# Four mixers in a row: the next mixer's norm is spread over the partitions behind the third part of its values, and the output projection's evictions stand behind all weight splits

## The chip, the cores and the metric

The kernel runs on one core of one Trainium2 chip. The metric is the device time of one execution in microseconds (us). TensorE (PE) multiplies, VectorE (DVE) and ScalarE (ACT) do the elementwise work and empty PSUM, GpSimd (POOL) helps, and SyncE (SP) issues nearly all transfers.

## The reference, cut to what matters

A first model of two blocks (mixers and a mixture of experts) is followed by a second one of four mixers in a row. Only the second one is touched by the change:

```python
def second_block(x, norm_pre, norm_post, ...):
    h = x
    for i in range(4):
        u = rms_norm_2(h, norm_pre[i])                     # over the 1024 channels of each of 256 tokens
        y = (nsa_mixer, diff_mixer, dilated_mixer, stick_mixer)[i](u, ...)
        h = h + rms_norm_2(y, norm_post[i])
    return h

def diff_mixer(u, w_in, w_out, ...):                       # the other mixers have the same frame
    q, k, v, z = split_cols(u @ w_in, (1024,) * 4)
    ...                                                    # attention gives o, 256 x 1024
    return (o * jax.nn.silu(z)) @ w_out
```

## The kernel before

All matrices are float32. A product of two float32 matrices is made of three matmuls: each operand is split into a rounded high part and the low rest (`wh` and `wl` for weights, `oh` and `ol`, `rawh` and `rawl` for activations), and high by low, low by high and high by high are added up in PSUM. A weight of 1024 x 256 comes by one transfer of 1 MB (`wload`, L220, a pool of five buffers), and `split` makes its halves: for each half, ACT rounds (L248, the cast `wh<-w`), then DVE subtracts (L249, `wl<-w,wh`). There are four buffers each of `wh` and `wl`, of half a weight each, so that two weights are split at any time, and a cast waits until TensorE has done with the weight that held its buffer.

The 256 tokens lie as two tiles of 128 rows in `h` (`hrow` in the trace). A mixer ends in `out_proj`: four column blocks of 256 of the product with `w_out`, for two row tiles t. Each piece is evicted by ACT (L354, squares summed into `ssq`) and by DVE (L355, times the gain, into `y`); both read the same PSUM bank and so take turns. `norm` makes the scale of a row tile of `ssq` (`rout`: a reduction on DVE, then Ln and Exp on ACT), and `add` puts y times the scale on `h` (L360). The next mixer does not wait for its own norm: `rows_turned` turns the rows into columns on TensorE (L404) and splits the result, times the gain of the next norm, into `rawh` and `rawl` without the row's scale (L409 on ACT, L410 on DVE), first row tile 0. Row tile 1 and the scale itself are made by `next_norm` (kept in `self.rest`), which `values` calls after the first eight of its products.

`values` is the next mixer's first product, v = u @ w (L608), in four column blocks, called the four parts here. The first two parts have their weights ready (`self.ahead`); row tile 0 is done for both before row tile 1. The scale `rc` is put on at the eviction of v (L632, L633). The q, k and z products, which have tokens along the free dimension, need the scale along the free dimension as well, as `rr` and `rq`: `rb` is `rc` spread to 128 columns (L428), two transposes turn it (L431), and two copies take it out of PSUM (L432, L433).

The order of the instructions on each engine is not written out. A scheduler sorts them by a simulated timeline; the code's order and `issue_after(ins)`, which keeps what is traced inside it behind `ins` on the engine of `ins`, constrain it. Within an engine the order is then fixed.

The places where one mixer ends and the next begins are called the three transitions: into `diff` (from about 1107 us), into `dilated` (from about 1261 us) and into `stick` (from about 1396 us). `stick` ends the program with an `out_proj` that writes the output.

Of the kernel before, what the change touches and what calls it, by code (L numbers as in the profile page):

```python
# [11 lines left out]
F32R = mybir.dt.float32r  # L12
BF16 = mybir.dt.bfloat16
I32 = mybir.dt.int32
AF = mybir.ActivationFunctionType
# [4 lines left out]
S = 256  # L20
D = 1024
KT = 8
# [85 lines left out]
class K:  # L108
# [227 lines left out]
    def out_proj(self, pool, oh, ol, w_out, gain, ahead=None, out=None):  # L336

        nc, h = self.nc, self.h  # L340
        y = pool.tile([128, 2, D], F32, name="y", tag="v")
        junk = pool.tile([128, 512], F32, name="ysq", tag="ysq")
        ssq = pool.tile([128, 2, 4], F32, name="ssq")
        r = pool.tile([128, 2], F32, name="rout")

        def product(v, t, w, ks, first=True, last=True):
            for k in ks:
                for j, (o, b) in enumerate(((oh, 1), (ol, 0), (oh, 0))):
                    nc.tensor.matmul(v, o[:, k, 128 * t:128 * t + 128], w[b][k], start=first and k == 0 and j == 0,  # L349
                                     stop=last and k == KT - 1 and j == 2)  # L350

        def evict(v, t, c):
            cs = slice(256 * c, 256 * c + 256)
            nc.scalar.activation(junk[:, :256], v, AF.Square, accum_out=ssq[:, t, c:c + 1])  # L354
            nc.vector.tensor_mul(y[:, t, cs], v, gain[:, cs])  # L355

        def add(t, b):
            cs = slice(512 * b, 512 * b + 512)
            dst = h if out is None else y
            nc.vector.scalar_tensor_tensor(dst[:, t, cs], y[:, t, cs], r[:, t:t + 1], h[:, t, cs], op0=ALU.mult, op1=ALU.add)  # L360
            if out is not None:
                nc.sync.dma_start(out[128 * t:128 * t + 128, cs], y[:, t, cs])

        weights = lambda c: self.wsplit(w_out[:, 256 * c:256 * c + 256], after=self.oh_last if c == 2 else (), pool_too=c == 1)

        half = slice(0, 256), slice(256, 512)
        ws, p = [weights(0), weights(1)], [self.mm(), self.mm()]
        for ks in ((0, 1, 2, 3), (4, 5), (6, 7)):
            for c in range(2):
                for t in range(2):  # L370
                    product(p[t][:, half[c]], t, ws[c], ks, c == 0, c == 1)
        w, q = weights(2), self.pss()
        for ks in ((0, 1, 2, 3), (4, 5, 6, 7)):
            for t in range(2):
                product(q[:, half[t]], t, w, ks, t == 0, t == 1)
        w = weights(3)
        for t in range(2):
            for c in range(2):
                evict(p[t][:, half[c]], t, c)
        for t in range(2):  # L380
            evict(q[:, half[t]], t, 2)
        if ahead is not None:
            self.ahead = [self.wsplit(ahead[0][0])]
            self.raw = [x.tile([128, KT, S], F32R, name=n, tag=n) for x, n in ((self.rawh, "rawh"), (self.ub, "rawl"))]
        p = [self.pss()[:, :256] for _ in range(2)]
        for t in range(2):
            product(p[t], t, w, range(KT))
        for t in range(2):
            evict(p[t], t, 3)
            self.norm(r[:, t:t + 1], ssq[:, t])  # L390
            for b in range(2):
                add(t, b)
                if ahead is not None and t == 0:
                    self.rows_turned(ahead[1], t, b)
        if ahead is not None:
            self.ahead += [self.wsplit(a) for a in ahead[0][1:]]
            self.rest = lambda: self.next_norm(ahead[1])

    def rows_turned(self, gain, t, b):
# [13 lines left out]
    def next_norm(self, gain):  # L413

        nc, h = self.nc, self.h
        for b in range(2):
            self.rows_turned(gain, 1, b)

        self.rc, self.rr, self.rq = (self.hp.tile([128, n], F32, name=t, tag=t) for t, n in (("rc", 2), ("rr", S), ("rq", S)))
        hsq = self.hp.tile([128, 2, 2], F32, name="hsq", tag="hsq")  # L420
        with self.tc.issue_after(self.raw_last[0]):
            for t in range(2):
                for b in range(2):
                    junk = self.ub.tile([128, 2, S], F32, name="rawsq", tag="rawsq", bufs=2)
                    nc.scalar.activation(junk.rearrange("p a b -> p (a b)"), h[:, t, 512 * b:512 * b + 512], AF.Square, accum_out=hsq[:, t, b:b + 1])
                self.norm(self.rc[:, t:t + 1], hsq[:, t])
        rb = self.ub.tile([128, 2, S], F32, name="rb", tag="rawsq", bufs=2)[:, :, :128]
        nc.vector.tensor_copy(rb, self.rc.unsqueeze(2).to_broadcast([128, 2, 128]))  # L428
        p = self.pst()
        for t in range(2):  # L430
            nc.tensor.transpose(p[:, 128 * t:128 * t + 128], rb[:, t], self.ident)  # L431
        nc.scalar.copy(self.rr, p[:, :S])  # L432
        nc.scalar.mul(self.rq, p[:, :S], 0.125)  # L433

    def norm(self, out, parts):

        nc = self.nc
        nc.vector.tensor_reduce(out, parts, axis=mybir.AxisListType.X, op=ALU.add)
        nc.scalar.activation(out, out, AF.Ln, bias=self.eps, scale=1.0 / D)
        nc.scalar.activation(out, out, AF.Exp, scale=-0.5)  # L440

    def normed(self, wk, p, r, n=2):

# [155 lines left out]
    def values(self, parts):  # L599

        nc = self.nc
        x = self.raw
        ps = [self.mm(), self.mm()] + (self.pair() if len(parts) > 2 else [])

        def product(i, w, t, k):
            ts = slice(128 * t, 128 * t + 128)
            for j, (a, b) in enumerate(((0, 1), (1, 0), (0, 0))):
                last = nc.tensor.matmul(ps[i][:, 256 * t:256 * t + 256], x[a][:, k, ts], w[b][k], start=k == 0 and t == 0 and j == 0,  # L608
                                        stop=k == KT - 1 and t == 1 and j == 2).ins
            return last  # L610

        ws = self.ahead
        self.ahead = None

        tiles = range(2)
        order = ([(i, t, k) for t in tiles for i in range(2) for k in range(KT)] if self.by_tile else
                 [(i, t, k) for k in range(KT) for i in range(2) for t in tiles])
        for n, (i, t, k) in enumerate(order):
            if n == KT and self.rest is not None:
                with self.tc.issue_after(last):  # L620
                    self.rest()
                self.rest = None
            last = product(i, ws[i], t, k)
        (last_a, last_b), rc = self.raw_last, self.rc
        for i, (src, v) in enumerate(parts):
            if i > 1:
                with self.tc.issue_after(last_a), self.tc.issue_after(last_b):
                    w = self.wsplit(src)
                for t in tiles:
                    for k in range(KT):  # L630
                        product(i, w, t, k)
            nc.scalar.mul(v[:, 0], ps[i][:, :256], rc[:, 0:1])  # L632
            nc.vector.tensor_scalar(v[:, 1], ps[i][:, 256:], rc[:, 1:2], None, op0=ALU.mult)  # L633

# [600 lines left out]
    def even(self, gs, shift, gate):  # L1235
# [3 lines left out]
        with ExitStack() as ctx:  # L1239
# [71 lines left out]
            with self.pool("eo", 1) as op:  # L1311
                add, norm = self.norms(self.blk, op, 2)
                for c in range(4):
                    w = self.wload(w_out[:, 256 * c:256 * c + 256])
                    with self.tc.issue_after(self.last):
                        w = self.split(w)
                    for m in range(2):
                        k = 2 * c + m
                        p = self.mm()
                        sl = slice(128 * m, 128 * m + 128)  # L1320
                        self.gemm(p, lambda k: w[0][k][:, sl], lambda k: w[1][k][:, sl], lambda k: xs[k // 2][0][:, k % 2], lambda k: xs[k // 2][1][:, k % 2],
                                  (4, 5, 6, 7, 0, 1, 2, 3))
                        for i, dst in ((0, self.x), (1, self.cx)):
                            nc.vector.scalar_tensor_tensor(dst[:, k], p[:, 256 * i:256 * i + 256], gate[:, k, i:i + 1],
                                                           dst[:, k], op0=ALU.mult, op1=ALU.add)
                        add(k, [self.x[:, k], self.cx[:, k]])
                self.r = norm()
# [963 lines left out]
```

## Time and profile before

| what | value |
|---|---|
| median of 3 runs | 1564.4 us (1552.34 to 1564.49) |
| the profiled execution: time, span of its trace | 1566.07 us, 1564.4 us |
| mean granted clock of TensorE over the span | 0.955 |
| PE busy | 1417.6 us (91%) |
| DVE, ACT, POOL busy | 967.4, 807.1, 253.8 us (62%, 52%, 16%) |
| mean transfer rate | 183 GB/s |

Busy time is an average over stages with different limits. What a change in one place is worth is read from the stretch around it: which engine waits there, and for what.

### The profile page before, as it was taken

The numbers are of one execution on the slowest core, as the hardware profiler recorded it, in microseconds if no ns is written. First come the engines' busy times: TensorE is split into PE (matmuls) and PEld (weight loads), VectorE is DVE, ScalarE is ACT, GpSimd is POOL, SyncE is SP. The second block draws the span as 40 slices with busy tenths as digits, with TensorE's granted clock in tenths as the row PEclk, the third lists the DMA queues.
The fourth block names the chain that finished last, engine by engine and source line by source line (L and its number), as shares of the span: only waits on it lengthen the run. The fifth ranks groups of instructions, "written<-read, shape, count | busy, mean of one in ns | idle before, by whom it ended". The sixth has DMA issues, their size and how long they took to land.

```text
span 1564.4 us, 26543 instructions
## 1 busy us (share of the span) xinstructions
PE 1417.6 (91%) x10345; PEld 1150.0 (74%) x10345; DVE 967.4 (62%) x2107; ACT 807.1 (52%) x1665; POOL 253.8 (16%) x245
## 2 busy tenths in 40 slices
PE   5989987889599898998799989999799989988997
PEld 3767865566387775766566669987799879888997
DVE  4555669763577665876412347886667755765775
ACT  4455545543366553665212244675646764755574
POOL 2000115322211103101100002121001100400232
PEclk7999999999699998999899989998999999999999
DMA  8700359865699996413979947421544355434420
GB/s 267 239 27 1 96 171 290 267 222 186 186 306 341 342 339 215 151 59 116 315 264 363 361 141 223 137 64 48 172 146 133 115 184 173 151 127 135 143 74 28
DMA packets 244122, 286.29 MB, mean 183 GB/s; under 512 B 14595, under 2 KB 227603, under 8 KB 243989
## 3 DMA queue, kind: packets, MB, share of 16 engines
q1 hardware_dynamic: 237076, 261.43, 51.5%
q0 software_dynamic: 6912, 23.07, 4.5%
q8 instruction: 85, 1.39, 0.4%
q14 instruction: 49, 0.39, 0.1%
HBM read 277.13 MB, written 9.44 MB: 183 GB/s over the span
## 4 chain that ended last, share of the span: by engine, by line
PE 40%; DVE 4%; ACT 3%; DMA 1%; issue 1%; POOL 1%; another core or an unknown queue 0%; SPq 0%; DVEq 0%; POOLq 0%
PE ps_mm L261 6%; PE ps_mm L263 5%; PE ps_mm L262 5%; PE ps_mm L2043 3%; PE ps_x L349 3%; PE ps_x L608 2%; PE ps_x L471 2%; PE ps_mm L349 2%; PE ps_t L2083 2%; PE ps_mm L608 1%; PE ps_x L500 1%; PE ps_o L510 1%; DVE wl L249 1%; PE ps_t L2026 1%; DMA w<-exp_w_up 1%
## 5 line engine op out<-in xcount | busy, mean ns | idle before, releaser
L249 DVE TENSOR_TENSOR wl<-w,wh 128x1024 fp32r<-128x1024 f32 x258 | 314.0, 1226 | 175.6 <-ACT wh L248 173.2
L248 ACT CAST wh<-w 128x1024 fp32r<-128x1024 f32 x262 | 269.8, 1040 | 187.4 <-PE ps_mm L263 93.8
L261 PE MATMUL ps_mm<-rawh,wl 128*128 128x256 f32 x720 | 206.2, 286 | 0.0
L262 PE MATMUL ps_mm<-rawl,wh 128*128 128x256 f32 x720 | 206.0, 286 | 0.0
L263 PE MATMUL ps_mm<-rawh,wh 128*128 128x256 f32 x720 | 204.9, 285 | 0.0
L263 PEld LDWEIGHTS ps_mm<-rawh,wh 128*128 128x128 f32 x720 | 137.1, 190 | 2.8 <-issue 1.8
L261 PEld LDWEIGHTS ps_mm<-rawh,wl 128*128 128x128 f32 x720 | 136.2, 189 | 2.5 <-issue 0.7
L262 PEld LDWEIGHTS ps_mm<-rawl,wh 128*128 128x128 f32 x720 | 136.5, 190 | 1.6 <-issue 0.6
L261 PE MATMUL ps_mm<-wh,xl 128*96 128x256 f32 x256 | 76.0, 297 | 2.8 <-DVE xl L462 2.8
L262 PE MATMUL ps_mm<-wl,xt 128*96 128x256 f32 x256 | 74.5, 291 | 0.0
L263 PE MATMUL ps_mm<-wh,xt 128*96 128x256 f32 x256 | 73.4, 287 | 0.0
L1094 PE MATMUL ps_mm<-w,cond 128*32 128x256 f32 x768 | 57.2, 415 | 16.3 <-DVE mod L1101 10.3
L2125 PE MATMUL ps_s<-w,ht 128*96 128x512 f32 x128 | 57.7, 593 | 0.0
L2043 PE MATMUL ps_mm<-w,xt 128*64 128x256 f32 x384 | 51.6, 384 | 0.0
L1094 PEld LDWEIGHTS ps_mm<-w,cond 128*32 128x32 f32 x768 | 22.7, 115 | 38.7 <-DVE mod L1101 13.2
L261 PE MATMUL ps_mm<-hh,wl 128*128 128x512 f32 (+2 forms) x136 | 47.5, 351 | 2.9 <-DVE qn L1138 2.6
L261 PEld LDWEIGHTS ps_mm<-wh,xl 128*96 128x96 f32 x256 | 42.9, 168 | 7.0 <-DVE xl L462 3.8
L262 PE MATMUL ps_mm<-hl,wh 128*128 128x512 f32 (+2 forms) x136 | 47.4, 349 | 0.3 <-DVE hl L1119 0.2
L263 PE MATMUL ps_mm<-hh,wh 128*128 128x512 f32 (+2 forms) x136 | 46.8, 344 | 0.0
L1540 POOL TENSOR_TENSOR xk<-d,KD 128x512 f32<-128x512 f32 x27 | 39.5, 1469 | 33.3 <-PE ps_x L1547 16.5
L262 PEld LDWEIGHTS ps_mm<-wl,xt 128*96 128x96 f32 x256 | 42.9, 168 | 0.8 <-issue 0.8
L263 PEld LDWEIGHTS ps_mm<-wh,xt 128*96 128x96 f32 x256 | 43.0, 168 | 0.3 <-issue 0.3
(630 smaller groups left out, 3895.9 us busy)
## 6 DMA issues: line engine op xcount, KB each, us to landing
w<-mod_w SPq DMA_DIRECT2D x48, 1024.0 KB, 6.8
w<-exp_w_up SPq DMA_DIRECT2D x28, 1024.0 KB, 11.0
w<-exp_w_gate SPq DMA_DIRECT2D x27, 1024.0 KB, 12.3
w<-exp_w_down SPq DMA_DIRECT2D x27, 1024.0 KB, 11.4
w<-b_w_in SPq DMA_DIRECT2D x16, 1024.0 KB, 5.5
w<-d_w_in SPq DMA_DIRECT2D x16, 1024.0 KB, 5.5
w<-a_w_in SPq DMA_DIRECT2D x14, 1024.0 KB, 9.8
w<-c_w_in SPq DMA_DIRECT2D x14, 1024.0 KB, 5.1
```

Source lines behind the costliest of these rows:

```text
L248: nc.scalar.copy(hv, raw[:, i:i + c])
L249: (nc.gpsimd if i and pool_too else nc.vector).tensor_sub(lv, raw[:, i:i + c], hv.bitcast(F32))
L261: nc.tensor.matmul(out, sl(k), mh(k), start=k == ks[0], stop=False)
L262: nc.tensor.matmul(out, sh(k), ml(k), start=False, stop=False)
L263: nc.tensor.matmul(out, sh(k), mh(k), start=False, stop=k == ks[-1])
L349: nc.tensor.matmul(v, o[:, k, 128 * t:128 * t + 128], w[b][k], start=first and k == 0 and j == 0, stop=last and k == KT - 1 and j == 2)
L471: self.nc.tensor.matmul(out, q[a], k[b], start=j == 0, stop=j == 2)
L608: last = nc.tensor.matmul(ps[i][:, 256 * t:256 * t + 256], x[a][:, k, ts], w[b][k], start=k == 0 and t == 0 and j == 0, stop=k == KT - 1 a ...
L1094: nc.tensor.matmul(p[j:j + 32, :256], self.cond[:, k], w[:, k], start=k < 4, stop=k >= 4)
L1540: nc.gpsimd.tensor_mul(xk, d, Ks)
L2043: nc.tensor.matmul(p[64 * a:64 * a + 64, 256 * j:256 * j + 256], xt[:, k, off + 64 * a:off + 64 * a + 64], w[j][a][k], start=k == 0, stop= ...
L2125: nc.tensor.matmul(p, ht[:, f], w[:, f, cs], start=f == 0, stop=f == 1)
```

## The change

In `out_proj`, the last column block's product and the splitting of the next mixer's first weight are issued ahead of all evictions, and the evictions are then issued row tile by row tile, each tile's norm and addition behind its own four pieces. The next mixer's second weight is kept behind the scale of row tile 0 (its second half also behind the splitting of the turned rows of tile 0). In `next_norm` the scales of both row tiles are made by one `norm` on two columns in place of two. The spreading of the scale (`rb`, the two transposes, `rr` and `rq`) leaves `next_norm` and becomes `norm_spread`, which `values` calls after the product of the third part.

```diff
@@ out_proj
         w = weights(3)
+        if ahead is not None:
+            self.ahead = [self.wsplit(ahead[0][0])]
+            self.raw = [x.tile([128, KT, S], F32R, name=n, tag=n) for x, n in ((self.rawh, "rawh"), (self.ub, "rawl"))]
+        l = [self.pss()[:, :256] for _ in range(2)]
+        for t in range(2):
+            product(l[t], t, w, range(KT))
         for t in range(2):
             for c in range(2):
                 evict(p[t][:, half[c]], t, c)
-        for t in range(2):
             evict(q[:, half[t]], t, 2)
-        if ahead is not None:
-            self.ahead = [self.wsplit(ahead[0][0])]
-            self.raw = [x.tile([128, KT, S], F32R, name=n, tag=n) for x, n in ((self.rawh, "rawh"), (self.ub, "rawl"))]
-        p = [self.pss()[:, :256] for _ in range(2)]
-        for t in range(2):
-            product(p[t], t, w, range(KT))
-        for t in range(2):
-            evict(p[t], t, 3)
-            self.norm(r[:, t:t + 1], ssq[:, t])
+            evict(l[t], t, 3)
+            i = self.norm(r[:, t:t + 1], ssq[:, t])
+            scale = i if t == 0 else scale
             for b in range(2):
                 add(t, b)
                 if ahead is not None and t == 0:
                     self.rows_turned(ahead[1], t, b)
+                    first = self.raw_last
         if ahead is not None:
-            self.ahead += [self.wsplit(a) for a in ahead[0][1:]]
+            with self.tc.issue_after(scale):
+                self.ahead += [self.wsplit(a, after=first) for a in ahead[0][1:]]
             self.rest = lambda: self.next_norm(ahead[1])
@@ next_norm
-                self.norm(self.rc[:, t:t + 1], hsq[:, t])
+            self.norm(self.rc, hsq)
+
+    def norm_spread(self):
+
+        nc = self.nc
         rb = self.ub.tile([128, 2, S], F32, name="rb", tag="rawsq", bufs=2)[:, :, :128]
         nc.vector.tensor_copy(rb, self.rc.unsqueeze(2).to_broadcast([128, 2, 128]))
         p = self.pst()
@@ values
             if n == KT and self.rest is not None:
                 with self.tc.issue_after(last):
                     self.rest()
-                self.rest = None
+                self.rest, spread = None, True
             last = product(i, ws[i], t, k)
...
                 for t in tiles:
                     for k in range(KT):
-                        product(i, w, t, k)
+                        last = product(i, w, t, k)
+                if i == 2 and spread:
+                    with self.tc.issue_after(last):
+                        self.norm_spread()
```

The scheduler's result differs only at the three transitions and in the last `out_proj`. Three places of the first transition follow; the other two transitions have the same rows with other buffer numbers.

On TensorE, in `values` of `diff`, where the first two parts end (`ps_mm`) and the third (`ps_x_11501`) begins, before:

```order
L608 MATMUL ps_mm_11500<-wl_11483,rawh_11384 128x256
L608 MATMUL ps_mm_11500<-wh_11482,rawl_11385 128x256
L608 MATMUL ps_mm_11500<-wh_11482,rawh_11384 128x256
L431 MATMUL ps_x_11573<-k_all_68,rb_11571 128x128 [waits DVE_49]
L431 MATMUL ps_x_11573<-k_all_68,rb_11571 128x128
L608 MATMUL ps_x_11501<-wl_11657,rawh_11384 128x256
L608 MATMUL ps_x_11501<-wh_11656,rawl_11385 128x256 [waits Activation_49]
```

The same place of the changed kernel:

```order
L613 MATMUL ps_mm_11500<-wh_11482,rawh_11372 128x256
L613 MATMUL ps_x_11501<-wl_11647,rawh_11372 128x256 [waits DVE_49]
L613 MATMUL ps_x_11501<-wh_11646,rawl_11373 128x256 [waits Activation_49]
...
L613 MATMUL ps_x_11501<-wh_11650,rawh_11372 128x256
L436 MATMUL ps_x_11704<-k_all_68,rb_11702 128x128 [waits DVE_49]
L436 MATMUL ps_x_11704<-k_all_68,rb_11702 128x128
L613 MATMUL ps_x_11502<-wl_11714,rawh_11372 128x256
```

The two transposes of `rb` stood ahead of the 48 matmuls of the third part and now stand behind them, ahead of the fourth part (`ps_x_11502`).

On ScalarE, around the scale of row tile 0 at the end of `out_proj` (`ps_mm_11196` holds row tile 1's first two column blocks, `ps_x_11386` tile 0's last one, `wh_11478` is the first half of the next mixer's second weight), before:

```order
L354 ACTIVATE ysq_11172,ssq_11173<-ps_x_11386 128x256 [waits PE_49,Activation_49]
L248 CAST wh_11478<-w_11476 128x1024 [waits DMAHW6_49,PE_49]
L439 ACTIVATE rout_11174<-rout_11174,eps_76 128x1 [waits DVE_49]
L440 ACTIVATE rout_11174<-rout_11174 128x1 [waits Activation_49]
L354 ACTIVATE ysq_11172,ssq_11173<-ps_x_11387 128x256 [waits PE_49]
L248 CAST wh_11482<-w_11476 128x1024
```

The same place of the changed kernel, where tile 0's last column block is `ps_x_11374`:

```order
L354 ACTIVATE ysq_11172,ssq_11173<-ps_x_11374 128x256 [waits PE_49,Activation_49]
L354 ACTIVATE ysq_11172,ssq_11173<-ps_mm_11196 128x256 [waits Activation_49]
L444 ACTIVATE rout_11174<-rout_11174,eps_76 128x1 [waits DVE_49]
L354 ACTIVATE ysq_11172,ssq_11173<-ps_mm_11196 128x256 [waits DVE_49]
L445 ACTIVATE rout_11174<-rout_11174 128x1 [waits Activation_49]
L248 CAST wh_11478<-w_11476 128x1024 [waits DMAHW6_49,PE_49]
```

The cast has moved behind the scale's Exp (now L445), and the two evictions of row tile 1, which stood further ahead, now surround its Ln (now L444). The cast of the second half, `wh_11482`, has moved behind the eight splits of tile 0's turned rows.

On VectorE, between the addition of row tile 0 and the first low part of the turned rows, the changed kernel has:

```order
L360 SCALAR_TENSOR_TENSOR hrow_9137<-y_11171,rout_11174,hrow_9137 128x512 [waits DVE_49]
L249 TENSOR_TENSOR wl_11479<-w_11476,wh_11478 128x1024 [waits DMAHW6_49,Activation_49]
L355 TENSOR_TENSOR y_11171<-ps_x_11303,gain_9165 128x256 [waits Activation_49]
L355 TENSOR_TENSOR y_11171<-ps_x_11375,gain_9165 128x256 [waits Activation_49]
L443 TENSOR_REDUCE rout_11174<-ssq_11173 128x1
L411 SCALAR_TENSOR_TENSOR rawl_11373<-ps_x_11436,cols_mix_213,rawh_11372 128x128 [waits Activation_49]
```

Before, one eviction, the reduction and the split of the second half (`wl_11483`) stood there; the split of the first half stood ahead of the addition. Now two evictions of row tile 1 stand there, and the first half's split.

## Rows read from the trace of the kernel before

**Rows 1.** The page: the chain that ended last, by engine.
```profile
PE 40%; DVE 4%; ACT 3%; DMA 1%; issue 1%; POOL 1%; another core or an unknown queue 0%; SPq 0%; DVEq 0%; POOLq 0%
```

**Rows 2.** Waits of TensorE, first transition: total us, times, longest.
```profile
PE ps_x L431 <- DVE rb L428: 4.6, 1, 4.6
PE ps_x L404 <- DVE hrow L360: 1.7, 1, 1.7
PE ps_mm L608 <- DVE rawl L410: 1.6, 2, 0.9
```

**Rows 3.** Waits of TensorE, second transition.
```profile
PE ps_x L431 <- DVE rb L428: 4.1, 1, 4.1
```

**Rows 4.** Waits of TensorE, third transition.
```profile
PE ps_x L431 <- DVE rb L428: 4.7, 1, 4.7
```

**Rows 5.** TensorE's timeline, first transition: start us, us, instruction, [idle before].
```profile
1114.65 0.37 PE L608 MATMUL ps_mm<-wh,rawl 128*128 128x256 f32 x1
...
1124.98 0.28 PE L608 MATMUL ps_mm<-wh,rawh 128*128 128x256 f32 x1
1129.84 0.69 PE L431 MATMUL ps_x<-k_all,rb 128*128 128x128 f32 x2 [4.57 <-DVE rb L428]
1130.18 0.56 PE L608 MATMUL ps_x<-wl,rawh 128*128 128x256 f32 x1
1130.54 0.42 PE L608 MATMUL ps_x<-wh,rawl 128*128 128x256 f32 x1
1130.75 0.41 PE L608 MATMUL ps_x<-wh,rawh 128*128 128x256 f32 x1
...
1136.04 0.28 PE L608 MATMUL ps_x<-wl,rawh 128*128 128x256 f32 x1
1136.15 0.28 PE L608 MATMUL ps_x<-wh,rawl 128*128 128x256 f32 x1
```

**Rows 6.** TensorE's timeline, second and third transition: first matmul behind the wait, first fast one.
```profile
1283.03 0.56 PE L608 MATMUL ps_x<-wl,rawh 128*128 128x256 f32 x1
...
1286.15 0.28 PE L608 MATMUL ps_x<-wh,rawh 128*128 128x256 f32 x1
...
1420.27 0.56 PE L608 MATMUL ps_x<-wl,rawh 128*128 128x256 f32 x1
...
1422.72 0.28 PE L608 MATMUL ps_x<-wh,rawh 128*128 128x256 f32 x1
```

**Rows 7.** Stretches: length, busy us of PE, PEld, DVE, ACT, POOL; PEclk, DMA share, GB/s.
```profile
1120.00:1126.00 6.00, 5.26 (x43) 5.02 (x42) 3.01 (x9) 5.72 (x16) 0.00 (x0) 1.00 0.00 0
1130.00:1132.00 2.00, 2.00 (x10) 2.00 (x11) 0.57 (x2) 0.66 (x2) 0.00 (x0) 0.50 1.08 381
1400.00:1402.00 2.00, 1.70 (x7) 1.35 (x6) 2.00 (x6) 0.75 (x4) 0.00 (x0) 0.50 0.30 77
```

**Rows 8.** VectorE's timeline, first transition.
```profile
1107.96 1.41 DVE L360 SCALAR_TENSOR_TENSOR hrow<-y,rout,hrow 128x512 f32<-128x512 f32 x2
...
1118.70 0.22 DVE L533 TENSOR_TENSOR lamp<-lam 64x2 f32<-64x2 f32 x1 [3.87 <-DMA lam<-b_lambda]
...
1124.34 1.23 DVE L249 TENSOR_TENSOR wl<-w,wh 128x1024 fp32r<-128x1024 f32 x1 [1.40 <-ACT wh L248]
...
1126.08 3.50 DVE L249 TENSOR_TENSOR wl<-w,wh 128x1024 fp32r<-128x1024 f32 x3 [0.46 <-ACT wh L248]
1129.49 0.29 DVE L428 COPY rb<-rc 128x256 f32<-128x256 f32 x1
```

**Rows 9.** ScalarE's timeline, first transition, around the scale of row tile 0.
```profile
1105.73 1.05 ACT L248 CAST wh<-w 128x1024 fp32r<-128x1024 f32 x1 [0.28 <-PE ps_x L349]
...
1107.01 0.20 ACT L440 ACTIVATE rout<-rout 128x1 f32<-128x1 f32 x1
```

**Rows 10.** VectorE's timeline, end of the program.
```profile
1557.10 1.41 DVE L360 SCALAR_TENSOR_TENSOR y<-y,rout,hrow 128x512 f32<-128x512 f32 x2 [0.60 <-ACT rout L440]
1558.54 0.42 DVE L355 TENSOR_TENSOR y<-ps_x,gain 128x256 f32<-128x256 f32 x1
...
1559.62 1.41 DVE L360 SCALAR_TENSOR_TENSOR y<-y,rout,hrow 128x512 f32<-128x512 f32 x2 [0.60 <-ACT rout L440]
```

More of the change, by code (lines that the diff above doesn't have):

```diff
@@ L439, in norm @@
         nc.scalar.activation(out, out, AF.Ln, bias=self.eps, scale=1.0 / D)
-        nc.scalar.activation(out, out, AF.Exp, scale=-0.5)
+        return nc.scalar.activation(out, out, AF.Exp, scale=-0.5).ins
     def normed(self, wk, p, r, n=2):
@@ L617, in values @@
                  [(i, t, k) for k in range(KT) for i in range(2) for t in tiles])
+        spread = False
         for n, (i, t, k) in enumerate(order):
```

## The prediction

> **What bounds the kernel now.** I read the chain of waits first. Two fifths of the span lie on it as TensorE's own work, the next engine has 4% [rows 1], so a microsecond counts where TensorE stands still. Then I read TensorE's waits in each of the three stretches that the change touches. Each has the same longest wait: the two transposes of `rb` (L431) wait for DVE's copy, 4.6, 4.1 and 4.7 us, once per transition [rows 2 to 4]. The first transition also has 1.7 us for the added rows `hrow` and 1.6 us for the low parts `rawl` of the turned rows [rows 2]. The timeline shows who is behind the longest wait: TensorE ends the first two parts at 1125.3, then stands until 1129.84, and behind the transposes come the matmuls of the third part, which need nothing of `rb` [rows 5]. DVE reaches `rb` only at 1129.49, behind four weight splits, of which the first ends at 1125.6 and the other three take until 1129.6 [rows 8]. So the third part, whose own first half-weight is split at 1125.6 and its second at 1127.2, is held by two transposes that nobody needs before the q product.
>
> The stand costs more than its length. Ahead of it the granted clock is 1.00, behind it 0.50, that is 1.2 in place of 2.4 GHz [rows 7]; matmuls then start 0.21 us apart (1130.54, 1130.75), and later 0.12 us apart [rows 5].
>
> **The change part by part.**
>
> *The spread behind the third part* removes the wait on `rb` from that place. The order shows the 48 matmuls of the third part now behind the second, and the transposes behind them. Terms: 4.6 + 4.1 + 4.7 = 13.4 us [rows 2 to 4]. Does the wait come back behind the third part? `rb` is ready at about 1129.8 today; the third part takes 48 x 0.12 = 5.8 us, so TensorE asks for `rb` at 1131 at the earliest, 1.2 us after it is there, and the reduction for both tiles at once saves an Ln and an Exp. I cost it at nothing. If that cover were gone, it would cost what `rb` is late, not 4.5 us. `rr` and `rq` come later by one part, but the first who needs them is the q product's eviction, a part (5.8 us) and a chunk behind. The transposes themselves stay on the path.
>
> *The clock behind the wait.* With no stand, I expect the third part at full clock. First transition: from 1130.18 to 1136.04 there are 27 steps (the first 0.36, 25 of 0.21, the last 0.17), 5.86 us [rows 5]; at 0.12 they would be 3.2, so 2.6 us come back. Second: 1283.03 to 1286.15, 14 steps, 3.1 against 1.7 us: 1.4. Third: 1420.27 to 1422.72, 11 steps, 2.45 against 1.3: 1.1 [rows 6]. Sum 5.1 us. The Trainium skill ("TensorE: Matmul & The Clock Gate", Part 1) puts it the same way round, the throttled clock is the default and activity releases it, and calls the number of slow matmuls variable from run to run; the trace agrees with 27, 14 and 11 slow steps behind nearly equal waits.
>
> *A new, smaller wait.* The third part now waits for its own weights: TensorE is done with the first two at 1125.3, first half split at 1125.6 [rows 5, 8], then 12 matmuls (1.4 us), second half at 1127.2: 0.3 and 0.2 us, if TensorE arrives as now; if it arrives earlier, more, unless the splits come earlier with it. They hang on ACT's chain of turned rows, which moves with it. Bounds 0 and 0.6 us per transition; I take 0.3, in all -0.9.
>
> *The front of the transition* (evictions, second weight behind the scale). On ACT the Exp of tile 0's scale ends at 1107.2, behind a cast of 1.05 us [rows 9] that now stands behind it. Two evictions of row tile 1 get in its way instead, each alternating with DVE. Laying the changed ACT and DVE rows end to end with the durations of today (cast 1.05, split 1.2, eviction 0.5 on ACT and 0.4 on DVE, addition 0.7) puts the addition at 1106.65, 1.3 us earlier than 1107.96 [rows 8]. But DVE then has a split and two evictions ahead of the first `rawl`, so the fourth block of turned rows reaches TensorE at 1114.1, against 1114.65 [rows 5]: 0.55 us are left, three times 1.65. The second weight's second half is now split behind tile 0's turned rows, ready at about 1116.3, just when TensorE has done its other matmuls and the eight transposes of tile 1: hidden, with almost no margin; a late one costs what it is late. In the first transition alone DVE stood 3.87 us for the transfer of `b_lambda` and held the `rawl` of tile 1 [rows 8]. In SP's queue that transfer stood behind a weight load that waits for the second half's split; it now stands ahead of that load, so it lands before DVE asks. From 1114.65 to 1124.98 TensorE needed 10.3 us [rows 5] for 75 matmuls and eight transposes, which at 0.12 and 0.1 are 9.7: 0.6 us to gain. Front: 2.3 us; bounds 0 (all given back to the splits) and 4.4 (the full 1.3 us three times, and half of the 1.7 us at half clock in the third transition [rows 7]). The weight load that SP now issues some 5 us later is the third behind the front, needed some 15 us on; nobody waits for it.
>
> The Trainium skill says of the queues of ScalarE and VectorE (same page, the table at its head) that they are strictly first in, first out. That speaks against moving the evictions, since all that stands ahead of the Exp holds it. If the Exp could pass them, the addition would begin about 0.6 us sooner, and the sum would gain 1.8 us more; I have counted the queue as it stands.
>
> *The end of the program.* The last `out_proj` has no next weight to hide evictions behind. Today the addition of tile 0 runs from 1557.10 and that of tile 1 from 1559.62, 1.08 us behind the start of the last eviction (1558.54) [rows 10]. In the new order two evictions of tile 1 delay tile 0's scale by up to 0.75 us, and two more stand behind the addition of 1.4 us: the last eviction starts at 1558.8 to 1559.6, the last addition at 1559.9 to 1560.7. That is 0.3 to 1.0 us longer; I take 1.0.
>
> **The sum.** 13.4 + 5.1 - 0.9 + 2.3 - 1.0 = 18.9 us. The profiled execution took 1566.1 us, 1.7 above the median shown: 1547.2 by its own time, 1545.5 beside the median of 1564.4. Behind each transition the chain runs on TensorE, and the transfers are triggered by releases that move with it, so I expect no give-back.
>
> **The rivals.**
>
> *A, the wait moves to the weights.* The third part waits for both halves of its weight, until 1127.2 [rows 8], because all that feeds the splits (turned rows, squares, casts) comes later than my sum has it. For: ACT is busy 5.72 of 6 us ahead of the wait [rows 7]. Against: the front leaves it more time. It would leave 2 us of each wait, 6 in all, and half the clock term (a 1.7 us wait kept the full clock in one transition, a shorter one lost it in another [rows 2, 7]): 13.4 - 6 + 2.5 - 1.0 = 8.9, 1555.5 us.
>
> *B, the clock falls in the front instead.* This ends slower. In the third transition short waits in the front alone brought the clock to 0.50 [rows 7]. If the scattered waits of the new front do this in all three, and the clock stays down through all 96 matmuls of the first two parts, it costs 96 x 0.09 = 8.6 us each, 26 in all, against the 18.9: 1571.5 us. It decides at about 70 slow matmuls per transition; below that the kernel is still faster. Against: the trace has no slow run above 27 steps here, and two of three fronts kept the full clock. The page named above would have the array fall back whenever activity is too sparse; by it this is possible, with the time just worked out, and nothing in these rows makes it likely.
>
> *C, the better run.* One of three runs shown took 1552.34, 12.1 us under the median, without any change; the clock's variation alone can do that. A changed kernel that keeps the clock up more often would sit there: 1552.3 - 18.9 = 1533.
>
> *D, the change does not do what it says:* excluded by the order, in which the transposes have moved at all three places.
>
> **How the numbers follow.** The forecast, between 1538 and 1552, has 0.60; A 0.22; B 0.06; C 0.12. The range reaches from C's 1533 to just above A's, 1557. About 1% (15.6 us, 1548.8) is what a measurement of this kernel can tell from no change. Faster by more: C and five sixths of the forecast, 0.62; within 1%: the rest of the forecast, A, and most of B, 0.35; slower: 0.03.
>
> **What would show it.** Right: no wait of TensorE on `rb` above 0.5 us in any transition, granted clock 1.00 in the third part, the time from the last matmul of `out_proj` to the end of the third part some 6 to 9 us shorter in each, and the end of the program up to 1 us longer. Wrong: a wait of 2 us or more on `wl` (L249) at the third part's first matmuls (A); 0.50 in all three fronts (B); a wait on `wl` just behind the transposes of row tile 1 (the hidden half-weight was not hidden).

## The result, and the profile after

The changed kernel takes 1539.7 us (median of 4 runs, 1538.1 to 1543.3) against 1564.2: a ratio of 0.9865 with a 95% interval of 0.9815 to 0.9914, that is 21 us less, between 13 and 29. Two further comparisons on other occasions gave 0.9865 (0.9836 to 0.9893) and 0.9852 (0.9827 to 0.9876). The forecast was 1545.5 us, 18.9 us less. Two executions were disturbed, one of 1797.8 us in the run without the spread's move and the profiled one of the last of these comparisons (2709.9 us); neither is read here, and no ratio counts them.

The profiled execution took 1538.13 us with a span of 1536.1 us. The waits of TensorE in the profile after, by line, tile and producer (total us, times, longest), here those of the first transition, which answer to [rows 2]:

```profile
PE ps_mm L613 <- DVE rawl L411: 1.5, 2, 0.9
PE ps_x L405 <- DVE hrow L360: 0.5, 1, 0.5
PE ps_mm L613 <- DVE wl L249: 0.2, 1, 0.2
```

The wait on `rb` is gone in all three transitions, and that on `hrow` fell from 1.7 to 0.5 us (in the other two from 1.6 to 0.4). The short wait on `wl` is new: it is the first half of the next mixer's second weight, which VectorE now splits behind the addition, and it lasts 0.2 to 0.3 us in each transition. It is not the sign of a hidden half-weight come late, since TensorE does not wait behind the transposes of row tile 1. Nothing took the place of the wait on `rb` at the start of the third part. TensorE's timeline there shows it, which answers to [rows 5] (start us, us, instruction, idle before):

```profile
1117.41 0.28 PE L613 MATMUL ps_mm<-wh,rawh 128*128 128x256 f32 x1
1117.53 0.31 PE L613 MATMUL ps_x<-wl,rawh 128*128 128x256 f32 x1
...
1118.86 0.28 PE L613 MATMUL ps_x<-wh,rawh 128*128 128x256 f32 x1
1119.02 0.39 PE L613 MATMUL ps_x<-wl,rawh 128*128 128x256 f32 x1
...
1123.24 0.28 PE L613 MATMUL ps_x<-wh,rawh 128*128 128x256 f32 x1
1123.36 0.38 PE L436 MATMUL ps_x<-k_all,rb 128*128 128x128 f32 x2
1123.50 0.36 PE L613 MATMUL ps_x<-wl,rawh 128*128 128x256 f32 x1
```

The third part (`ps_x`) begins 0.12 us behind the last matmul of the second, one plain step. The steps stay at 0.12 us, and only 0.04 us are lost at 1119.02, where the second half of its weight begins. Busy time and granted clock in the third part of each transition, which answer to [rows 7] (length, busy us of PE, PEld, DVE, ACT, POOL; PEclk, DMA share, GB/s):

```profile
1118.00:1120.00 2.00, 2.00 (x18) 1.92 (x17) 2.00 (x2) 1.97 (x4) 0.00 (x0) 1.00 0.00 0
1262.00:1264.00 2.00, 2.00 (x19) 2.00 (x18) 1.73 (x3) 2.00 (x4) 0.00 (x0) 1.00 0.00 0
1391.00:1393.00 2.00, 2.00 (x19) 2.00 (x19) 1.73 (x3) 2.00 (x4) 0.00 (x0) 1.00 0.00 0
```

All three stand at 1.00. Before, the first had 0.50 there [rows 7], and the other two began with 14 and 11 slow steps [rows 6]. VectorE's timeline of the first transition answers to [rows 8]:

```profile
1100.59 1.40 DVE L360 SCALAR_TENSOR_TENSOR hrow<-y,rout,hrow 128x512 f32<-128x512 f32 x2
...
1109.78 0.15 DVE L538 TENSOR_TENSOR lamp<-lam 64x2 f32<-64x2 f32 x1
...
1116.17 1.23 DVE L249 TENSOR_TENSOR wl<-w,wh 128x1024 fp32r<-128x1024 f32 x1 [2.42 <-ACT wh L248]
...
1117.74 3.50 DVE L249 TENSOR_TENSOR wl<-w,wh 128x1024 fp32r<-128x1024 f32 x3 [0.27 <-ACT wh L248]
1121.15 0.29 DVE L433 COPY rb<-rc 128x256 f32<-128x256 f32 x1
```

`rb` still comes behind four weight splits, but it is there at 1121.4 and TensorE asks at 1123.36: 2 us to spare. The stand for `b_lambda` (3.87 us ahead of `lamp`) is gone.

**Where the time came from.** I took four marks from the starts of TensorE's rows: the last matmul of `out_proj`, the last matmul of the second part, and the first ones of the third and the fourth part. The first mark of the first transition, before, and after with the fourth block of turned rows behind it (before: 1114.65 [rows 5]):

```profile
1106.84 0.28 PE L349 MATMUL ps_x<-wh,oh 128*128 128x256 f32 x1
```

```profile
1100.74 0.28 PE L349 MATMUL ps_x<-wh,oh 128*128 128x256 f32 x1
...
1107.60 0.36 PE L613 MATMUL ps_mm<-wh,rawl 128*128 128x256 f32 x1
```

Between the marks, in us, for the three transitions:

| stretch | before | after | gain |
|---|---|---|---|
| last of `out_proj` to last of the second part (front) | 18.14, 17.59, 18.98 | 16.67, 17.12, 16.71 | 4.2 |
| to the first of the third part (wait on `rb`, transposes) | 5.20, 4.75, 5.33 | 0.12, 0.12, 0.12 | 14.9 |
| to the first of the fourth part | 8.33, 7.13, 6.81 | 5.97, 5.98, 5.97 | 4.4 |
| whole | 31.67, 29.47, 31.12 | 22.76, 23.22, 22.80 | 23.5 |

The end gives 0.9 us back (below), and the stretches between the transitions agree within 0.4 us, so the change itself is worth 22.6 us in the traces. The two spans differ by 28.3 us: 0.4 us were lost between the transitions, and 6.1 us lie ahead of the first one, where both kernels issue the same instructions: the last matmul of that `out_proj` began at 1106.8 before and at 1100.7 after, and in the nine other traces that are read here anywhere from 1102.6 to 1108.3. The difference does not arise in one place: by the rows of TensorE that both traces have, the changed kernel is 1.5 us ahead at 187 us, 4.5 at 520 us and 6.1 at 982 us. I put it down to chance.

### The profile page after: what moved, and what is told of

Read it like the earlier page. It is cut to its first block, busy times and chain, and to the rows that moved or that the text cites. A ratio compares the mean times of both kernels' runs of the same rounds, so it can differ in the third digit from the quotient of the medians.

```text
span 1536.1 us, 26539 instructions
## 1 busy us (share of the span) xinstructions
PE 1407.5 (92%) x10345; PEld 1142.8 (74%) x10345; DVE 967.9 (63%) x2104; ACT 806.5 (53%) x1659; POOL 254.9 (17%) x245
```

## The experiments

The traces of the experiments are read with the same marks. A ratio is always to the kernel before, on the same chip.

**The changed kernel again.** No edit.

> The changed kernel once more, beside the kernel before on the same chip. Theory (the terms of the prediction, re-read from the two traces): what changes between the end of out_proj's last product and the start of the fourth part gives 23.5 us (8.9, 6.3 and 8.3), the end of the program takes back 0.9 us, the 5.8 us left of the 28.3 us between the two spans lie ahead of the first transition, where both kernels issue the same instructions, and are chance: the ratio is 0.985 to 0.987, 1540 to 1544 us against 1564. Rival (the change helps elsewhere too): 28 us again, a ratio of 0.982, with the 6 us ahead of 1107 us again.

Measured: ratio 0.9865 (0.9836 to 0.9893), 68.97 us in the three transitions (68.78 in the first trace), and the last matmul of the first transition's `out_proj` at 1102.6. The theory holds: the 6 us ahead of 1107 us are not the change's.

**The spread alone**, in the kernel before:

```diff
@@ next_norm, values (kernel before)
+    def norm_spread(self):
...
         rb = self.ub.tile([128, 2, S], F32, name="rb", tag="rawsq", bufs=2)[:, :, :128]
...
+                if i == 2 and spread:
+                    with self.tc.issue_after(last):
+                        self.norm_spread()
```

> The kernel before with the spread alone moved behind the third part; evictions, weight splits and both norms as before. Theory (each term stands by itself): the waits on rb go (14.9 us with the transposes at half clock), the clock behind them comes back (4.3 us), and in their place TensorE waits 0.3 to 0.6 us in each transition for the splits of the third part's own weight: 17.5 us faster, 1546.5 us, and the time from out_proj's last matmul to the fourth part falls from 31.7, 29.5 and 31.1 to about 25, 24 and 26 us. Rival (the wait moves to the weights, since the front is as late as before): 2 us of each wait on wl stay and half the clock term: 10 to 11 us faster, 1553 us, with waits of L608 on L249 of 1.5 us or more.

Measured: ratio 0.9895 (0.9866 to 0.9924), 16.4 us; in the trace 24.85, 24.59 and 25.67 us, 17.15 us less than before. TensorE's waits on the third part's weight, first and second transition (the third has none that is listed):

```profile
PE ps_x L612 <- DVE wl L249: 0.3, 1, 0.3
...
PE ps_x L612 <- DVE wl L249: 0.7, 1, 0.7
```

The wait does not move to the weights, not even with the old front. What shows there is the small wait of the prediction: all that stands between the last matmul of the second part and the fourth part beyond the 6.1 us of the changed kernel adds up to 1.9 us over the three transitions.

**Everything but the spread's move**, from the changed kernel:

```diff
-    def norm_spread(self):
...
-                if i == 2 and spread:
-                    with self.tc.issue_after(last):
-                        self.norm_spread()
```

> The changed kernel with the spread back in its old place, ahead of the third part (evictions, weight splits, one norm for both tiles as changed). In the trace after, rb was copied 20.4 us behind out_proj's last matmul and TensorE had done the first two parts 16.8 us behind it: so a wait of about 3.9 us is expected here, against 4.1 to 4.7. Theory (the front's gain stands by itself): the front gives its 4.2 us and the wait is 0.5 us shorter per transition, the clock behind it falls as before, the end costs 0.9 us: 4.5 to 5 us faster, 1559.5 us. Rival (what the front gains is given back at the wait on rb, since rb does not come earlier): waits of 5.5 to 6 us, nothing gained, 1564 to 1565 us.

Measured: ratio 0.9965 (0.9943 to 0.9987), 5.5 us. TensorE's longest wait in the first transition, and the clock behind it in all three:

```profile
PE ps_x L432 <- DVE rb L429: 3.8, 1, 3.8
```

```profile
1126.00:1128.00 2.00, 1.76 (x8) 1.77 (x9) 0.97 (x3) 0.66 (x2) 0.00 (x0) 0.50 1.06 371
1277.00:1279.00 2.00, 1.59 (x10) 1.59 (x11) 1.14 (x4) 0.66 (x2) 0.00 (x0) 0.76 1.09 381
1411.00:1413.00 2.00, 1.30 (x6) 1.30 (x7) 1.43 (x4) 0.68 (x3) 0.00 (x0) 0.54 0.99 326
```

The wait is 3.8 us in each transition, as expected; the transitions are 6.8 us shorter than before, and the end takes 0.9 back. The front's gain is not given back at `rb`, and it adds to the spread's: 17.15 + 6.83 = 24.0 us against 23.5 for both.

**Work in the place of the stand**, in the kernel before (the spread is kept between the second and the third part):

```diff
...
+        if spread:
+            with self.tc.issue_after(last):
+                for n in range(34):
+                    last = nc.tensor.matmul(ps[2][:, :256], x[0][:, n % KT, :128], x[0][:, (n + 1) % KT], start=True, stop=True).ins
+            with self.tc.issue_after(last):
+                turned = self.norm_spread()
...
```

> The kernel before with 34 matmuls of no use (128x256, into the bank of the third part before it starts) between the second part and the transposes of rb: 4 us of work in the place of the stand, the output is not touched. Theory (the clock falls because TensorE stands): the wait on rb falls to 0.7 us or less, the third part runs at 1.00 at once, and the 4.3 us of the clock term come back although rb comes no earlier: 4 us faster, 1560 us. Rival (the clock falls for another reason, such as the load of the other engines or the float32 transposes): the third part starts at 0.50 again with 11 to 27 slow steps, and the time stays at 1564 us.

Measured: ratio 0.9955 (0.9934 to 0.9975), 7 us less. Clock and busy time behind the transposes in the three transitions:

```profile
1131.00:1133.00 2.00, 1.89 (x16) 1.89 (x17) 0.84 (x3) 0.66 (x2) 0.00 (x0) 1.00 1.09 381
1282.00:1284.00 2.00, 1.59 (x14) 1.59 (x15) 1.14 (x4) 0.66 (x2) 0.00 (x0) 1.00 1.09 384
1416.00:1418.00 2.00, 1.96 (x17) 1.86 (x17) 0.88 (x3) 0.66 (x2) 0.00 (x0) 1.00 1.08 381
```

`rb` comes about as late as before (its copy begins 22.5, 22.9 and 21.7 us behind `out_proj`'s last matmul, against 22.7, 21.7 and 23.6), the wait on it is 0.6 us or less, and the transfers run at 381 to 384 GB/s, as before [rows 7]. Yet the third part runs at 1.00 and takes 5.74 us in each transition, where it took 8.33, 7.13 and 6.81: 5.05 us. It is the stand that brings the clock down. This also isolates the clock term. The whole is 6.4 us shorter in the trace, 2.4 more than the 4 us that I expected from the clock alone. 1.05 of that is the clock term, and 1.3 lie ahead of the third part, where the second transition lost 1.1 us, as `rb` came 1.2 us later, and the third won 2.1 us, as it came 1.9 us earlier: their fronts fell to half clock at other places than in the kernel before.

**The spread inside the third part**, behind 24 of its 48 matmuls (`n == 7`) or 12 (`n == 3`), the rest of them kept behind the transposes:

```diff
...
+                    with ExitStack() as rest:
+                        if turned is not None:
+                            rest.enter_context(self.tc.issue_after(turned))
+                        last = product(i, w, t, k)
+                    if i == 2 and spread and n == 7:
+                        with self.tc.issue_after(last):
+                            turned = self.norm_spread()
```

> The changed kernel with the spread behind the first half (24 of 48 matmuls) of the third part. With the spread ahead of the third part the transposes began 20.8 us behind out_proj's last matmul; TensorE gets here 19.6 us behind it. Theory (a stand costs its length, and the clock only falls behind a long one: behind the 1.7 us for hrow at the first transition it stayed at full speed, behind 3.8 us it fell): a wait of 1.1 us in each transition, the second half at 1.00: 3.5 us slower than the changed kernel. Rival (any stand brings the clock down): 1.1 us, and 0.50 for all of the second half, 2.3 us more in each: 10 us slower.

> The same behind a quarter (12 of 48 matmuls) of the third part, where TensorE gets 18.2 us behind out_proj's last matmul. Both theories: a wait of 2.5 us in each transition. If the clock still holds here, 7.5 us slower than the changed kernel; if it falls as it did behind 3.8 us (10 to 20 slow steps of 0.09 us), 10 to 13 us slower. With the run of 24 it says between which two lengths of this stand the fall lies.

Measured behind 24: a wait of 0.8 us in each transition, the clock at 1.00 in all three, 71.9 us, 3.0 us more than the changed kernel; ratio 0.9876 (0.985 to 0.9902). Behind 12: a wait of 2.4 us in each, and two answers. Three stretches that begin within each of the waits, the first, the second and the third transition:

```profile
1123.00:1126.00 3.00, 2.55 (x22) 2.55 (x23) 1.18 (x4) 0.66 (x2) 0.00 (x0) 1.00 1.04 349
1270.00:1273.00 3.00, 2.29 (x15) 2.29 (x16) 1.44 (x4) 0.78 (x3) 0.00 (x0) 0.80 1.07 369
1403.00:1406.00 3.00, 2.77 (x24) 2.77 (x25) 0.96 (x3) 0.66 (x2) 0.00 (x0) 1.00 1.07 364
```

In the second transition alone the clock fell, and 16 steps were slow; the transitions took 25.3, 26.8 and 25.4 us, 8.6 us more than the changed kernel, ratio 0.9927 (0.9896 to 0.9958). So the rival (any stand brings the clock down) is out, and equal stands can end both ways.

**The hold taken away**, from the changed kernel:

```diff
-            with self.tc.issue_after(scale):
-                self.ahead += [self.wsplit(a, after=first) for a in ahead[0][1:]]
+            self.ahead += [self.wsplit(a) for a in ahead[0][1:]]
```

> The changed kernel without the hold on the next mixer's second weight: its casts stand again where the scheduler puts them, the first ahead of the Exp of row tile 0's scale. Theory (the front's gain comes from that cast standing behind the Exp): the wait on hrow rises from 0.4 to 1.7 us, as before, part of it comes back since the low parts rawl no longer stand behind that weight's split: 0.5 to 1.3 us per transition, 1.5 to 4 us slower than the changed kernel. Rival (the order of the evictions makes the gain, the hold is idle): 0.4 us on hrow, the same time.

Measured: ratio 0.9907 (0.9887 to 0.9927), by the ratios 6.6 us more than the changed kernel's 0.9865. ScalarE's timeline at the end of the first `out_proj`, which answers to [rows 9], in the changed kernel (Exp, then the cast):

```profile
1100.11 0.19 ACT L445 ACTIVATE rout<-rout 128x1 f32<-128x1 f32 x1
1100.20 1.04 ACT L248 CAST wh<-w 128x1024 fp32r<-128x1024 f32 x1
```

The same here (Ln, the cast, Exp), and the waits of TensorE there:

```profile
1102.97 0.29 ACT L443 ACTIVATE rout<-rout,eps 128x1 f32<-128x1 f32 x1
1103.30 1.05 ACT L248 CAST wh<-w 128x1024 fp32r<-128x1024 f32 x1
1104.26 0.20 ACT L444 ACTIVATE rout<-rout 128x1 f32<-128x1 f32 x1
```

```profile
PE ps_x L404 <- DVE hrow L360: 1.7, 1, 1.7
PE ps_mm L612 <- DVE rawl L410: 1.4, 1, 1.4
```

The cast stands between Ln and Exp again and the wait on `hrow` is back at 1.7 us, as the theory has it. The size was wrong: I expected 1.5 to 4 us, and the transitions are 7.6 to 7.8 us longer (76.6 against 69.0 and 68.8). The low parts do not make up for it, they come later too (a wait of 1.4 us), and the second half of the third part's weight, 0.04 us late in the changed kernel, now costs a wait of 0.4 us. The clock falls as well, to 0.61 in the stretch behind the two waits:

```profile
1110.00:1114.00 4.00, 4.00 (x23) 3.81 (x22) 2.98 (x8) 1.50 (x5) 0.00 (x0) 0.61 1.03 344
```

**The old order of evictions with the hold**, from the changed kernel: the evictions of `out_proj` as they were, all else as changed.

> The changed kernel with all evictions of out_proj in the old order and place; the hold on the next mixer's second weight, the spread behind the third part and the one norm for both tiles stay. Theory (the hold makes the front's gain, the new order of evictions only puts two evictions of row tile 1 in the way of tile 0's scale): the addition starts 0.2 to 0.4 us earlier still relative to out_proj's last matmul, so 0.4 us or less between TensorE's last product and its first transposes' wait, 22.3 to 22.8 us per transition against 22.8 to 23.2, and 0.9 us less at the end: about 2 us faster than the changed kernel, ratio 0.984 or 0.985. Rival (the order of the evictions carries the gain and the hold only keeps it from being lost): the wait on hrow is 1.7 us again, 24.5 us or more per transition: 4 us slower than the changed kernel.

> The changed kernel beside the run with the old order of evictions, on the same chip. By the theory there it is 2 us slower than that run, by the rival 4 us faster; by itself a ratio of 0.9865 to the kernel before, as in the two comparisons so far, with 68.8 to 69.0 us in the three transitions.

Measured: ratios 0.9845 (0.982 to 0.9869) and 0.9852 (0.9827 to 0.9876), which the times cannot tell apart. The trace can: 22.56, 22.38 and 22.36 us, 67.3 in all against 68.8 and 69.0, and the end as in the kernel before. VectorE's addition of row tile 0 and the wait on it:

```profile
1103.60 1.41 DVE L360 SCALAR_TENSOR_TENSOR hrow<-y,rout,hrow 128x512 f32<-128x512 f32 x2 [0.60 <-ACT rout L447]
```

```profile
1104.49 1.29 PE L407 MATMUL ps_x<-k_all,hrow 128*128 128x128 f32 x8 [0.34 <-DVE hrow L360]
```

The last matmul of `out_proj` began at 1103.87 there, so the addition starts 0.27 us ahead of it, against 0.15 us ahead in the changed kernel and 1.12 us behind it before. The front is 49.0 us over the three transitions with the hold and the old order, 50.5 with the hold and the new order, 56.6 with the new order alone, and 54.7 (before) or 54.9 (the spread alone) with neither. The hold makes the front's gain; the new order of evictions by itself costs 1.5 to 1.9 us. Two things were not run by themselves. The hold keeps two casts, one behind the Exp and one behind the turned rows; the rows above point at the first, but no run parts them. And the one norm for both tiles, which is in all the runs from the changed kernel, has no run of its own.

**The old end**, from the changed kernel, for the last `out_proj` alone:

```diff
+        if ahead is None:
+            for t in range(2):
+                for c in range(2):
+                    evict(p[t][:, half[c]], t, c)
+            for t in range(2):
+                evict(q[:, half[t]], t, 2)
...
```

> The changed kernel, with the last out_proj alone (no next weight) in the old order of evictions. Theory (the end term): from the start of TensorE's last matmul to the start of the last addition it was 1.90 us before and is 2.84 us after; here it falls back to 1.9 us and the program gains 0.9 us, which the median cannot show (ratio 0.986, as the changed kernel). Rival (the end is set by something else, such as the output's transfer): 2.8 us there, or 1.9 us with an end that comes no earlier behind the last matmul.

Measured: TensorE's last matmul and VectorE's last addition, here:

```profile
1530.50 0.28 PE L349 MATMUL ps_x<-wh,oh 128*128 128x256 f32 x1
```

```profile
1532.41 1.41 DVE L360 SCALAR_TENSOR_TENSOR y<-y,rout,hrow 128x512 f32<-128x512 f32 x2 [0.60 <-ACT rout L452]
```

That is 1.91 us. In the changed kernel it is 2.84 us:

```profile
1528.52 0.28 PE L349 MATMUL ps_x<-wh,oh 128*128 128x256 f32 x1
```

```profile
1531.36 1.41 DVE L360 SCALAR_TENSOR_TENSOR y<-y,rout,hrow 128x512 f32<-128x512 f32 x2 [0.60 <-ACT rout L445]
```

The span ends 7.6 us behind the last matmul there against 6.7 us here. The end term is 0.9 us. The time, 1538.5 us, ratio 0.9831 (0.9808 to 0.9854), is better by more than that; but its interval overlaps that of the changed kernel, and the transitions, 68.94 us, are as there, so nothing shows that the rest is more than chance.

## Why the prediction was right, step by step

- *The spread.* Right. The waits on `rb` and the transposes at half clock were worth 14.9 us (13.4 forecast for the waits). No wait came back behind the third part: `rb` is there 1.9 us before TensorE asks, where I had 1.2. Only the transposes stay on the path, as said, 0.23 us in each transition at full clock. The move alone gives 17 us with the clock term.
- *The clock behind the wait.* Right in mechanism and size: 5.1 us forecast from counted slow steps, 5.05 us measured with work in the place of the stand.
- *The new, smaller wait.* Mis-sized, 0.9 forecast, 0.1 measured. With the old front it is there (1.9 us); the new front brings the splits earlier by more than it brings TensorE, which I had not worked out. The margin is thin: the second half is 0.04 us late.
- *The front.* Mis-sized, 2.3 forecast, 4.2 measured, inside its bounds of 0 to 4.4 (the two terms named for the upper bound, 3.9 and half of 1.7, make 4.75). The addition did come 1.3 us earlier, but I let the split and the evictions on VectorE take 0.75 us of it back each time. In the first transition they took 0.3: counted from the last matmul of `out_proj`, the fourth block of turned rows comes 0.95 us earlier (forecast 0.55), and the rest of the front is 0.5 us shorter (forecast 0.6). By the table the first transition kept 1.5 us and the third 2.3, since its clock stayed up; only the second gave some back and kept 0.5, with half clock in its front, which the run with the old end does not have there (16.69 us). I also took the gain for that of evictions and hold together; the runs give it to the hold, and a small loss to the evictions. The stand for `b_lambda` went, as said, and the half-weight behind the turned rows was hidden.
- *The end.* 1.0 forecast, 0.9 measured.
- *The rivals.* A (the wait moves to the weights) is out, shown by the spread alone. B (the clock falls in the front) did not decide: in the profile after it shows in the second transition alone, and costs a part of the 0.8 us that its front gave back. But the run without the hold shows that its mechanism is real: there the clock fell behind front waits of 1.7 and 1.4 us. In the kernel before it stayed at 1.00 in the first transition behind waits of 1.7, 0.8 and 0.9 us, so their sum alone does not decide. C is in part what the first profile shows: 6 us of its 28 were the run's luck.

The sum: 18.9 us forecast, 22.6 us in the traces, 21 us in the times.

## What to carry to other kernels

When an engine with a strict order waits, look at what is queued behind the wait: moving two small transposes behind work that needs nothing of them gave more than their wait, since the clock behind the stand came back too. Take an edit of several parts apart on the engines' queues: here the hold on one weight's two casts made the whole gain of the front, and the new order of evictions that came with it cost a little. Read gains of this size between marks inside the trace, since the same instructions ahead of the change vary by up to 7.6 us from run to run.

## What the runs showed that I had not expected

Behind the 2.35 us stand of the second transition (spread behind 12 matmuls) the clock did not fall at once. TensorE started eight matmuls within 0.9 us at full speed, and then the steps doubled:

```profile
1270.71 0.44 PE L436 MATMUL ps_x<-k_all,rb 128*128 128x128 f32 x2 [2.35 <-DVE rb L433]
1270.91 0.36 PE L614 MATMUL ps_x<-wl,rawh 128*128 128x256 f32 x1
...
1271.70 0.30 PE L614 MATMUL ps_x<-wl,rawh 128*128 128x256 f32 x1
1271.82 0.39 PE L614 MATMUL ps_x<-wh,rawl 128*128 128x256 f32 x1
1272.01 0.42 PE L614 MATMUL ps_x<-wh,rawh 128*128 128x256 f32 x1
1272.23 0.42 PE L614 MATMUL ps_x<-wl,rawh 128*128 128x256 f32 x1
```

So a slow row need not stand right behind the wait that caused it. Why one of three equal stands ended so is open.
